# One decoder layer on one core: the out stage goes by token halves, activation sums are made before the transposes, staged weight sums are made sooner

## The chip, the cores and the metric

The kernel runs on one NeuronCore of one Trainium2 chip. The core has five engines, each with its own instruction stream: TensorE (PE; its weight loads are PEld in the profile), VectorE (DVE), ScalarE (ACT), GpSimd (POOL) and SyncE (SP), whose queue issues the DMAs here. The metric is the device time of the one core in microseconds (us).

## The reference

One layer, 1024 tokens, width 1024, all in float32. The parts that this change touches come after the token mixing, which leaves `merged`:

```python
    h = h + rmsnorm(merged @ w_out[i], mix_post_norm[i])
    f = rmsnorm(h, ffn_pre_norm[i])
    f = jnp.square(jax.nn.relu(f @ w_ff_in[i])) @ w_ff_out[i]
    h = h + rmsnorm(f, ffn_post_norm[i])
    e = (p[i] @ w_ple[i]) * jax.nn.sigmoid(h @ w_ple_gate[i])
    h = h + rmsnorm(e, ple_post_norm[i])
```

`w_out` is 1024 x 1024, `w_ff_in` 1024 x 4096, `w_ff_out` 4096 x 1024. `rmsnorm` divides by the root mean square of a row and multiplies by a gain.

## The kernel before

**Arithmetic.** Every float32 operand is split into a high part (fp32r, an ACT copy) and a low part (value minus high, on DVE or POOL), and each product is three matmuls (`mm3`, lines 292, 294, 296): high-high, high-low, low-high. Nearly every other instruction of ACT, DVE, POOL and SP is recorded through a wrapper, at line 113 for the compute engines and 132 for DMAs, so the profile's groups are told apart by tile names.

**Order.** PE's order is made at build time by a planner (`Order`): a list of dense bodies (matmuls) into which chains (generators that wait, then emit a few instructions) are woven by estimated times; `t_f[i]` is the planner's time at which tile `i` of `f` is ready, and `done` its list of events. A wait in it orders the instructions; no engine executes it. PE then works strictly in that order. ACT, DVE, POOL and SP are put in order by the framework, except where `manual_schedule` binds them to the order in which the code names them: SP alone from the start of `mlp`, all four (`OTHERS`) from the mixed pairs on.

**Out stage.** `merged` lies transposed in `mT` (high and low, one tile for each half of the tokens, tags `mth0`, `mtl0`, `mth1`, `mtl1`). `out_0(i)` multiplies token tile `i` (128 tokens) with the left 512 columns of `w_out` (`wo[0]`, in `TM0`, `TM1`) and `out_1(i)` with the right 512 (`wo[1]`, in `AR0`, `AR1`, `BK`, `UV`); each is a body of 24 matmuls of 128x512. All eight `out_0` come first, then all eight `out_1`. Behind each `out_1` the chain `mixed(i)` applies both norms and the residual (`x` is loaded by each `out_1` into `gn["x"]`), stores `h`, and calls `put_f(hh, i)`, which transposes the normalised tile on PE (`tp`) and writes the operands of the first MLP product, `f`. `F[1]` and `F[2]` are the halves of the width of the first 512 tokens; for the second 512 tokens `put_f` writes `F[3]` from the second half of the width, and from both halves the sums `F[4]` to `F[7]`.

**MLP.** Both products of the MLP are done in pairs of blocks by a seven-product scheme (Winograd's form of Strassen): `SEQ` and `MUL` name its products. The pair index `p` runs over 16 (`NP`). `mlp` works so:
- 27 *early* products (`early`, 12 matmuls each) of `F[1]`, `F[2]` with weights `wa` split three products ahead (`w1_split`, from `beside`), results to DRAM. `beside(j)` also makes, once the planner's clock is past `t_f[7]` + 2, steps of `ahead_`: it loads `w_ff_out` rows (`w2r`) for p = 4, 2, 0, forms four sums of blocks (`w2_sums`) and stores each split sum (`bs`, 0.5 MB) to DRAM.
- five *mixed pairs*: one product of p = 0 (`chunks`, `first`) and one early product each.
- for p from 1 to 15, the products of `first(p)` woven into the second MLP product of pair e = p - 1: for even e by `seven` (seven products, 84 matmuls, with `bs` sums fetched back as `duo`), for odd e by `plain` (eight steps `u`, 96 matmuls). Each weave carries 60 matmuls of `first`. In the odd-e loops the sums for the even p that follows are staged: `load_w2(p)`, then `w2_sums(p, 0..5)`, unless p is in `AHEAD` = (4, 2, 0). `take` loads earlier results (`hr`), `part` splits later weights through the `gst` tiles (`gp`, `gph`).

**Tags.** An `rtile` or `mtile` with a tag waits until the last reader of the tag's previous tile is done. The rows of `w_ff_out` for pair p take tags `("r", "k", "MP")[(2p + k) % 3]`, k = 0 and 1. `gst` has two buffers, PSUM has eight banks: `m0`, `m1` for transposes, `z0`, `z1`, `s0` by `zbank`, `s1` to `s3` by `bank`.

Of the kernel before, what the change touches and what calls it, by code (L numbers as in the profile page):

```python
# [244 lines left out]
def layer(ctx: ExitStack, tc: tile.TileContext, x, pT, wz, wup, w_out, wff1, w_ff2, w_ple, w_pleg,  # L245
# [58 lines left out]
    def wait(cond):  # L304
        while not cond():
            yield 0.1
# [930 lines left out]
    def mtile(p, h, shape, name, dt):  # L1237
        return mgpool().tile(shape, dt, name=name, tag=f"mt{p}{h}")
# [99 lines left out]
    def out_0(i):  # L1338
        def body():
            h, ts = tok(i)  # L1340
            if i == 0:
                gn["m"] = rtile([128, D], "gn", "a")
                SY.dma_start(gn["m"], gains[1:2, :].to_broadcast([128, D]))
            if i == 1:
                wo[1] = wo_half(1, GB)
            ps = zbank()
            yield from mm3(ps, [(mT[0][h][:, k, ts], mT[1][h][:, k, ts]) + wo[0][k] for k in range(KT)])
            if i % 2 == 0:
                y0[i // 2] = rtile([128, 2, 512], "y0", ("r", "k", "Ep", "En")[i // 2])
            y = y0[i // 2][:, i % 2]  # L1350
            V.tensor_tensor(y, ps, gn["m"][:, halves[0]], OP.mult)
            jk = rtile([128, 512], "jk", "gst")
            S.activation(jk, ps, AF.Square, accum_out=ss0[:, i:i + 1])
        sch.add(body)

    def out_1(i):
        def body():
            h, ts = tok(i)
            if i == 0:
                gn["f"] = rtile([128, D], "gn", "kk")  # L1360
                SY.dma_start(gn["f"], gains[2:3, :].to_broadcast([128, D]))
                gn["h"] = rtile([128, 2, 2, 512], "hh", "BT")
                gn["x"] = [rtile([128, D], "xt", t) for t in ("v", "px")]
                for n, tag in zip((1, 2), GA):
                    t = rtile([128, 2, 4, 512], "f", tag, F32R)
                    F[n] = t[:, 0], t[:, 1]
            if i in (5, 6):
                mlp_ahead(i - 5)
            ps = zbank()
            SY.dma_start(gn["x"][i % 2], x[i * 128:(i + 1) * 128, :])  # L1370
            yield from mm3(ps, [(mT[0][h][:, k, ts], mT[1][h][:, k, ts]) + wo[1][k] for k in range(KT)])
            sch.spawn(mixed(i, ps), 1)
        sch.add(body)

    gn = {}
    F = {}

    def ss2(srcs, jks):
# [17 lines left out]

    def mixed(i, ps):
        h = i // 4
        yield from wait(lambda: i == 0 or ("M", i - 1) in done and (i < 2 or i - 2 in t_f))
        xt = gn["x"][i % 2]  # L1400
        hh = [gn["h"][:, i % 2, c] for c in range(2)]
# [12 lines left out]
        yield sch.until(sch.dep + 0.3)  # L1414
        yield from wait(lambda: i < 5 or i - 1 in t_f)
        yield from put_f(hh, i)
        t_f[i] = sch.dep + 0.1

    def put_f(srcs, i):


        ts = slice((i % 4) * 128, (i % 4) * 128 + 128)
        if i == 4:
            for n, p, h in ((3, 0, 0), (7, 1, 0), (5, 0, 1), (6, 1, 1)):
                t = mtile("hl"[p], h, [128, 2, 4, 512], "f", F32R)
                F[n] = t[:, 0], t[:, 1]
            F[4] = [rtile([128, 4, 512], "f", tag, F32R) for tag in ("AR0", "AR1")]
        at = lambda n, x: F[n][x][:, :, ts]
        for b in range(2):
            ps, tag = yield from chain_bank([128, 4, 128], "tp")  # L1430
            for k in range(4):
                tr(ps[:, k, :], srcs[b][:, k * 128:(k + 1) * 128], 0.107)
            if i < 4:
                S.activation(at(1 + b, 0), ps, AF.Copy)
                V.tensor_tensor(at(1 + b, 1), ps, at(1 + b, 0), OP.subtract)
            elif b == 0:
                c = rtile([128, 4, 128], "c", "ex")
                S.activation(c, ps, AF.Copy)
            else:
                S.activation(at(3, 0), ps, AF.Copy)  # L1440
                V.tensor_tensor(at(3, 1), ps, at(3, 0), OP.subtract)
                d = rtile([128, 4, 128], "d", "py")
                V.tensor_tensor(d, ps, c, OP.subtract)
            sch.hold(tag)
        if i < 4:
            return
        t2, t4 = (rtile([128, 4, 128], n, tag) for n, tag in (("t2", "pg"), ("t4", "yc")))
        V.tensor_tensor(t2, d, at(1, 0), OP.add)
        V.tensor_tensor(t2, t2, at(1, 1), OP.add)
        G.tensor_tensor(c, c, at(1, 0), OP.subtract)  # L1450
        G.tensor_tensor(c, c, at(1, 1), OP.subtract)
        G.tensor_tensor(t4, at(2, 0), t2, OP.subtract)
        G.tensor_tensor(t4, t4, at(2, 1), OP.add)
        for n, x, eng in ((7, d, V), (6, t2, V), (5, c, G), (4, t4, G)):
            if n in (6, 5):
                yield 2.0
            S.activation(at(n, 0), x, AF.Copy)
            eng.tensor_tensor(at(n, 1), x, at(n, 0), OP.subtract)

    NP = FF // 256
    MUL = (1, 6, 5, 3, 7, 4, 2)
# [5 lines left out]

    def totals():  # L1470
        for m in range(2):
            t = rtile([128, 2, 4, 512], "tot", GA[m])
            tot.append([t[:, 0], t[:, 1]])

    def acc(i, c):
# [200 lines left out]
    def mlp():  # L1676
# [2 lines left out]
        while sch.t < t_f.get(3, 1e9):  # L1679
            yield 0.0  # L1680
        for j in range(NA):
            beside(j)
            yield from early(j)
        while sch.t < t_f.get(7, 1e9):
            yield 0.0
        last["turn"].__exit__(None, None, None)
        last["turn"] = tc.manual_schedule(engines=OTHERS)
        last["turn"].__enter__()
        A_["turn"] = True
        for n in range(5):  # L1690
            beside(NA + 2 * n)
            yield from chunks(4 * n + 4)
            beside(NA + 2 * n + 1)
            Y["j"] += 1
            yield from early(NA + 2 * n + 1)
            flush()
        prep(0)
        prep(1)
        for _ in range(4):
# [1 line left out]
        for p in range(1, NP):  # L1701
            Y["n"] = 0
            e = p - 1
            if e % 2 == 0:
                for x in range(7):
                    yield from chunks((20 * x + 23) // 7 if p < NP - 1 else (3, 6, 9, 13, 17, 20, 20)[x])
                    yield from seven(items.index((e, x)))
                    if x == 2:
                        load_w2(p)
                    if x == 4:  # L1710
                        take(p + 1)
                    if p == NP - 1:
# [11 lines left out]
            for u in range(8):  # L1724
# [1 line left out]
                    flush()  # L1726
                    part(2 * p - 4 + u // 2, 0)
                yield from chunks((20 * u + 23) // 8)
                if u == (2 if p in AHEAD else 0):
                    load_w2(p)  # L1730
                yield from plain(items.index((e, u // 2)), u % 2)
                if u == 3:
                    take(p + 1)
                if p in AHEAD:
                    if u == 3:
                        fetch(p, 6)
                else:
                    if u == 1:
                        w2_sums(p, 0)
                    if 0 < u < 6:  # L1740
                        w2_sums(p, u)
                if u % 2:
                    part(2 * p - 4 + u // 2, 1)
        for _ in range(4):
# [234 lines left out]
            P[f"p{n - 2}"] = [k2(t[:, 0]), k2(t[:, 1])]  # L1979

    def last_weights():
        P["wpg"] = [[mtile("hl"[p], 1 - c, [128, KT, 512], "wpg", F32R) for c in range(2)] for p in range(2)]
        P["g3"] = rtile([128, D], "g3", "v")
        SY.dma_start(P["g3"], gains[3:4, :].to_broadcast([128, D]))

# [244 lines left out]
```

## Time and profile before

| | us |
|---|---|
| median of 3 runs | 1799.94 (1799.66 to 1800.44) |
| the profiled execution | 1800.09 |
| its span in the profile | 1798.3 |
| out stage, first to last matmul of `w_out` | 895.7 to 988.7 |
| early products and mixed pairs, to the first `bk<-duo` | 988.7 to 1118.0 |
| `seven` and `plain`, to the last MLP pair | 1118.0 to 1651.9 |

Positions are from the span's start. In a row of the timeline stand start, duration, engine, line, operation, out<-in and count, and in brackets the idle time before it and what ended it. A matmul's duration includes its pipeline; what it costs in a dense row is the distance to the next start. A row of waits says which engine waited, for whom, how long in total, how often, and the longest.

### The profile page before, as it was taken

Reading aid. Unit: us, or ns where it says so; the run is one execution under the profiler, and the core shown is the slowest. Engines: PE = TensorE matmul, PEld = TensorE weight load, DVE = VectorE, ACT = ScalarE, POOL = GpSimd, SP = SyncE. Lnnn points to the kernel's source line nnn. Section 1 sums busy time; section 2 is a strip of 40 time slices with the busy share of each in tenths; the row PEclk is TensorE's granted clock in tenths of the full one; section 3 lists DMA queues with packets and bytes.
Section 4 is the critical chain, followed back from the end, with each engine's and each line's share of the span. In section 5 each row is a group of like instructions: output and inputs, shape, how many; then the busy total and the mean of one; then the engine's idle time right before and its main releaser. Section 6 shows DMA issues by size and latency. Waiting matters only on the chain.

```text
span 1798.3 us, 26359 instructions
## 1 busy us (share of the span) xinstructions
PE 1741.8 (97%) x10084; PEld 1410.6 (78%) x10084; DVE 1100.8 (61%) x1873; ACT 753.1 (42%) x1377; POOL 682.1 (38%) x458
## 2 busy tenths in 40 slices
PE   9999989999999999999999898999999999999998
PEld 8887877878877777778878686888878777787887
DVE  6289767677534333353727745766776777778743
ACT  5824433432344443543515565343333433334453
POOL 1344131231221323332310854665655656553211
PEclk9999999999999999999999999999999999999999
DMA  4621121213332222333504378554464464657611
GB/s 160 208 94 37 48 82 48 90 45 106 111 107 79 69 63 60 106 138 132 205 29 141 115 271 298 170 180 165 148 228 167 167 212 154 214 181 276 245 48 47
DMA packets 99969, 244.76 MB, mean 136 GB/s; under 512 B 11394, under 2 KB 11778, under 8 KB 99331
## 3 DMA queue, kind: packets, MB, share of 16 engines
q1 hardware_dynamic: 99842, 243.08, 39.3%
q8 instruction: 79, 1.29, 0.3%
q14 instruction: 48, 0.39, 0.1%
HBM read 169.24 MB, written 67.11 MB: 131 GB/s over the span
## 4 chain that ended last, share of the span: by engine, by line
PE 66%; DVE 9%; DMA 9%; ACT 5%; POOL 4%; issue 4%; SPq 2%; DVEq 0%; ACTq 0%; POOLq 0%
PE z L294 13%; PE z L296 13%; PE z L292 13%; PE bk L292 5%; PE bk L294 5%; PE bk L296 5%; SPq L132 2%; DMA w2r<-in_w_ff_dram 1%; DVE tot L113 1%; DMA duo<-bs 1%; PE sc L275 1%; DMA wa<-in_wff_dram 1%; DVE xy L113 1%; PE A L275 1%; PE y L275 1%
## 5 line engine op out<-in xcount | busy, mean ns | idle before, releaser
L292 PE MATMUL z<-uh,wh 128*128 128x512 f32 (+1 forms) x800 | 313.0, 391 | 6.2 <-ACT part L113 3.0
L294 PE MATMUL z<-ul,wh 128*128 128x512 f32 (+1 forms) x800 | 314.6, 393 | 1.3 <-DVE ul L113 1.3
L296 PE MATMUL z<-uh,wl 128*128 128x512 f32 (+1 forms) x800 | 313.3, 392 | 2.7 <-POOL wl L113 2.7
L113 POOL TENSOR_TENSOR wl<-wr,wh 128x1024 fp32r<-128x1024 f32 (+1 forms) x56 | 133.4, 2382 | 421.1 <-ACT wh L113 402.1
L113 DVE TENSOR_TENSOR tot<-tot,bk 128x512 f32<-128x512 f32 x336 | 219.6, 680 | 65.7 <-PE bk L296 65.4
L292 PEld LDWEIGHTS z<-uh,wh 128*128 128x128 f32 x800 | 151.5, 189 | 37.2 <-ACT part L113 3.5
L296 PEld LDWEIGHTS z<-uh,wl 128*128 128x128 f32 x800 | 151.6, 189 | 34.1 <-POOL wl L113 4.0
L294 PEld LDWEIGHTS z<-ul,wh 128*128 128x128 f32 x800 | 151.7, 190 | 32.4 <-issue 3.6
L113 ACT ACTIVATE wh<-wr 128x1024 fp32r<-128x1024 f32 (+2 forms) x94 | 81.0, 862 | 113.0 <-PE z L294 56.2
L113 ACT ACTIVATE hr<-hr 128x512 f32<-128x512 f32 x96 | 60.7, 632 | 133.2 <-DVE hr L113 131.7
L292 PE MATMUL bk<-duo 128*128 128x512 f32 x224 | 91.4, 408 | 14.9 <-DMA duo<-bs 8.9
L113 ACT ACTIVATE duo<-sum 128x512 fp32r<-128x512 f32 x64 | 40.0, 625 | 123.2 <-DVE sum L113 122.6
L294 PE MATMUL bk<-duo 128*128 128x512 f32 x224 | 89.6, 400 | 0.2 <-POOL duo L113 0.2
L296 PE MATMUL bk<-duo 128*128 128x512 f32 x224 | 89.4, 399 | 0.0
L292 PE MATMUL bk<-ws,duo 128*128 128x512 f32 x224 | 87.1, 389 | 0.0
L294 PE MATMUL bk<-ws,duo 128*128 128x512 f32 x224 | 87.1, 389 | 0.0
L296 PE MATMUL bk<-ws,duo 128*128 128x512 f32 x224 | 87.1, 389 | 0.0
L292 PE MATMUL z<-f,wh 128*128 128x512 f32 x212 | 83.1, 392 | 2.2 <-ACT pa L113 2.2
L296 PE MATMUL z<-f,wh 128*128 128x512 f32 x212 | 83.0, 392 | 0.0
L294 PE MATMUL z<-f,wh 128*128 128x512 f32 x212 | 82.9, 391 | 0.0
L113 POOL TENSOR_TENSOR wh<-wr,wh 128x512 fp32r<-128x512 f32 x38 | 53.9, 1421 | 67.3 <-ACT wh L113 55.8
L292 PEld LDWEIGHTS bk<-duo 128*128 128x128 f32 x224 | 43.3, 193 | 32.7 <-DVE tot L113 13.0
(366 smaller groups left out, 4113.3 us busy)
## 6 DMA issues: line engine op xcount, KB each, us to landing
wr<-in_wz_dram SPq DMA_DIRECT2D x48, 512.0 KB, 3.8
w2r<-in_w_ff_dram SPq DMA_DIRECT2D x34, 512.0 KB, 6.3
bs<-duo SPq DMA_DIRECT2D x32, 512.0 KB, 4.1
duo<-bs SPq DMA_DIRECT2D x32, 512.0 KB, 5.1
wr<-in_wff_dram SPq DMA_DIRECT2D x56, 256.0 KB, 4.1
hr<-p1scr SPq DMA_DIRECT2D x48, 256.0 KB, 4.7
xt<-in_x_dram SPq DMA_DIRECT2D x16, 512.0 KB, 3.7
gscr<-gst SPq DMA_DIRECT2D x32, 256.0 KB, 2.1
```

Of the source, the lines that this page charges most:

```text
L113: return f(*a, **kw)
L132: self.eng.dma_start(out_, in_)
L275: PE.matmul(out_, a, b, start=start, stop=stop)
L292: PE.matmul(ps, ah, bh, start=start and i == 0, stop=False, skip_group_check=not start)
L294: PE.matmul(ps, ah, bl, start=False, stop=False, skip_group_check=not start)
L296: PE.matmul(ps, al, bh, start=False, stop=i == n - 1, skip_group_check=not start)
```

## The change

- The bodies run as `out_0(0..3)`, `out_1(0..3)`, then `out_0(i)`, `out_1(i)` in turn for i = 4 to 7. `wo[1]` is prepared one body sooner, `out_0` takes its bank from `bank`, and `x` is loaded two tiles ahead from `mixed`.
- Each tile's normalised activations have a room of their own (`room_h`) instead of one of two. `F[1]`, `F[2]` and the totals `tot` move to the tags of `mT`'s first half, `F[3]`, `F[7]` to `TM0`, `TM1`; `wpg` follows.
- `put_f` for tiles 4 to 7 forms the sums in fp32 on the untransposed tiles `hhs[i - 4]` and `srcs`, and transposes all five operands; it no longer sums transposed operands. The transposes of a half are placed behind that half's last `out_1`.
- `ACT`, `DVE` and `POOL` are bound to the written order only after the five mixed pairs instead of before them.
- In `plain` loops the load for a p outside `AHEAD` moves to the end of the `seven` loop before, its six sum steps from u = 1, 1 to 5 to u = 0 to 3; `take` moves from u = 3 to 4, and the first `bs` fetch of such a p to u = 5.

```diff
@@ out_0 @@
-            if i == 1:
                 wo[1] = wo_half(1, GB)
-            ps = zbank()
+            ps = bank()
@@ out_1 @@
-                gn["h"] = rtile([128, 2, 2, 512], "hh", "BT")
+                hh = rtile([128, 2, 2, 512], "hh", "BT")
+                gn["h"] = [[hh[:, n, c] for c in range(2)] for n in range(2)]
...
-            if i in (5, 6):
-                mlp_ahead(i - 5)
+                for n in range(2):
+                    load_rows(n)
+            if i in (6, 7):
+                mlp_ahead(i - 6)
             ps = zbank()
-            SY.dma_start(gn["x"][i % 2], x[i * 128:(i + 1) * 128, :])
...
+            done.add(("O", i))
+    def load_rows(i):
+        SY.dma_start(gn["x"][i % 2], x[i * 128:(i + 1) * 128, :])
+    def room_h(i):
+        if i < 2:
+            return gn["h"][i]
+        if i in (3, 4):
+            return [rtile([128, 512], "hh", t) for t in (("ex", "py"), ("pg", "yc"))[i - 3]]
+        t = rtile([128, 2, 512], "hh", {2: "MP", 5: "r", 6: "k", 7: "Ep"}[i])
+        return [t[:, 0], t[:, 1]]
@@ mixed @@
-        yield from wait(lambda: i == 0 or ("M", i - 1) in done and (i < 2 or i - 2 in t_f))
+        yield from wait(lambda: i == 0 or ("M", i - 1) in done)
...
+        if i < 6:
+            load_rows(i + 2)
         yield sch.until(sch.dep + 0.3)
-        yield from wait(lambda: i < 5 or i - 1 in t_f)
+        yield from wait(lambda: (i == 0 or i - 1 in t_f) and ("O", 7 if i > 3 else 3) in done)
@@ put_f @@
+        if i == 0:
+            for n, p in ((1, 0), (2, 1)):
+                t = mtile("hl"[p], 0, [128, 2, 4, 512], "f", F32R)
+                F[n] = t[:, 0], t[:, 1]
...
-        t2, t4 = (rtile([128, 4, 128], n, tag) for n, tag in (("t2", "pg"), ("t4", "yc")))
-        V.tensor_tensor(t2, d, at(1, 0), OP.add)
-        V.tensor_tensor(t2, t2, at(1, 1), OP.add)
-        G.tensor_tensor(c, c, at(1, 0), OP.subtract)
-        G.tensor_tensor(c, c, at(1, 1), OP.subtract)
-        G.tensor_tensor(t4, at(2, 0), t2, OP.subtract)
-        G.tensor_tensor(t4, t4, at(2, 1), OP.add)
-        for n, x, eng in ((7, d, V), (6, t2, V), (5, c, G), (4, t4, G)):
...
+        todo = [(1, srcs[0]), (2, srcs[1])]
+        if i > 3:
+            a, b = hhs[i - 4], srcs
+            t2 = rtile([128, 512], "t2", "gst")
+            V.tensor_tensor(a[0], b[0], a[0], OP.subtract)
+            V.tensor_tensor(b[0], b[1], b[0], OP.subtract)
+            V.tensor_tensor(t2, b[1], a[0], OP.subtract)
+            G.tensor_tensor(a[1], a[1], t2, OP.subtract)
+            todo = [(3, b[1]), (5, a[0]), (7, b[0]), (6, t2), (4, a[1])]
+        for n, src in todo:
+            o = (slice(None), slice(None), ts)
             ps, tag = yield from chain_bank([128, 4, 128], "tp")
             for k in range(4):
+                tr(ps[:, k, :], src[:, k * 128:(k + 1) * 128], 0.107)
+            S.activation(F[n][0][o], ps, AF.Copy)
+            V.tensor_tensor(F[n][1][o], ps, F[n][0][o], OP.subtract)
             sch.hold(tag)
@@ beside @@
         if j == 20:
+            yield from wait(lambda: 7 in t_f)
             take(0)
@@ mlp @@
         while sch.t < t_f.get(7, 1e9):
             yield 0.0
+        for n in range(5):
+            yield from beside(NA + 2 * n)
+            yield from chunks(4 * n + 4)
+            yield from beside(NA + 2 * n + 1)
+            Y["j"] += 1
+            yield from early(NA + 2 * n + 1)
+            flush()
         last["turn"].__exit__(None, None, None)
         last["turn"] = tc.manual_schedule(engines=OTHERS)
         last["turn"].__enter__()
-        A_["turn"] = True
-        for n in range(5):
...
+                    if x == 6 and p < NP - 1 and p + 1 not in AHEAD:
+                        load_w2(p + 1)
...
-                if u == (2 if p in AHEAD else 0):
+                if u == 2 and p in AHEAD:
                     load_w2(p)
                 yield from plain(items.index((e, u // 2)), u % 2)
-                if u == 3:
+                if u == 4:
                     take(p + 1)
-                if p in AHEAD:
-                    if u == 3:
-                        fetch(p, 6)
-                else:
-                    if u == 1:
-                        w2_sums(p, 0)
-                    if 0 < u < 6:
-                        w2_sums(p, u)
+                if u == (3 if p in AHEAD else 5):
+                    fetch(p, 6)
+                if p not in AHEAD:
+                    for n in ((0,), (1, 2), (3, 4), (5,), (), (), (), ())[u]:
+                        w2_sums(p, n)
@@ end of layer @@
-    for i in range(8):
+    for i in range(4):
         out_0(i)
-    for i in range(8):
+    for i in range(4):
+        out_1(i)
+    for i in range(4, 8):
+        out_0(i)
         out_1(i)
```

More of the change, by code (lines that the diff above doesn't have):

```diff
@@ L1361, in body @@
                 SY.dma_start(gn["f"], gains[2:3, :].to_broadcast([128, D]))
-                gn["h"] = rtile([128, 2, 2, 512], "hh", "BT")
+                hh = rtile([128, 2, 2, 512], "hh", "BT")
+                gn["h"] = [[hh[:, n, c] for c in range(2)] for n in range(2)]
                 gn["x"] = [rtile([128, D], "xt", t) for t in ("v", "px")]
-                for n, tag in zip((1, 2), GA):
-                    t = rtile([128, 2, 4, 512], "f", tag, F32R)
-                    F[n] = t[:, 0], t[:, 1]
-            if i in (5, 6):
-                mlp_ahead(i - 5)
+                for n in range(2):
+                    load_rows(n)
+            if i in (6, 7):
+                mlp_ahead(i - 6)
             ps = zbank()
-            SY.dma_start(gn["x"][i % 2], x[i * 128:(i + 1) * 128, :])
             yield from mm3(ps, [(mT[0][h][:, k, ts], mT[1][h][:, k, ts]) + wo[1][k] for k in range(KT)])
             sch.spawn(mixed(i, ps), 1)
+            done.add(("O", i))
         sch.add(body)
+    def load_rows(i):
[7 more added lines that the diff above has]
+        return [t[:, 0], t[:, 1]]
     gn = {}
+    hhs = {}
     F = {}
@@ L1398, in mixed @@
         h = i // 4
-        yield from wait(lambda: i == 0 or ("M", i - 1) in done and (i < 2 or i - 2 in t_f))
+        yield from wait(lambda: i == 0 or ("M", i - 1) in done)
         xt = gn["x"][i % 2]
-        hh = [gn["h"][:, i % 2, c] for c in range(2)]
+        hh = hhs[i] = room_h(i)
         ss = small.tile([128, 1], F32, name="ss")
@@ L1422, in put_f @@
         ts = slice((i % 4) * 128, (i % 4) * 128 + 128)
+        if i == 0:
+            for n, p in ((1, 0), (2, 1)):
+                t = mtile("hl"[p], 0, [128, 2, 4, 512], "f", F32R)
+                F[n] = t[:, 0], t[:, 1]
         if i == 4:
-            for n, p, h in ((3, 0, 0), (7, 1, 0), (5, 0, 1), (6, 1, 1)):
-                t = mtile("hl"[p], h, [128, 2, 4, 512], "f", F32R)
+            for n, t in ((3, rtile([128, 2, 4, 512], "f", "TM0", F32R)), (7, rtile([128, 2, 4, 512], "f", "TM1", F32R)),
+                         (5, mtile("h", 1, [128, 2, 4, 512], "f", F32R)), (6, mtile("l", 1, [128, 2, 4, 512], "f", F32R))):
@@ L1426, in put_f @@
                 F[n] = t[:, 0], t[:, 1]
             F[4] = [rtile([128, 4, 512], "f", tag, F32R) for tag in ("AR0", "AR1")]
-        at = lambda n, x: F[n][x][:, :, ts]
-        for b in range(2):
+        todo = [(1, srcs[0]), (2, srcs[1])]
[7 more added lines that the diff above has]
+            todo = [(3, b[1]), (5, a[0]), (7, b[0]), (6, t2), (4, a[1])]
@@ L1430, in put_f @@
+        for n, src in todo:
+            o = (slice(None), slice(None), ts)
             ps, tag = yield from chain_bank([128, 4, 128], "tp")
             for k in range(4):
[L1432 to L1438, printed above, removed]
-            else:
[L1440 to L1443, printed above, removed]
@@ L1444, in put_f @@
-            sch.hold(tag)
-        if i < 4:
-            return
-        t2, t4 = (rtile([128, 4, 128], n, tag) for n, tag in (("t2", "pg"), ("t4", "yc")))
-        V.tensor_tensor(t2, d, at(1, 0), OP.add)
-        V.tensor_tensor(t2, t2, at(1, 1), OP.add)
-        G.tensor_tensor(c, c, at(1, 0), OP.subtract)
-        G.tensor_tensor(c, c, at(1, 1), OP.subtract)
-        G.tensor_tensor(t4, at(2, 0), t2, OP.subtract)
-        G.tensor_tensor(t4, t4, at(2, 1), OP.add)
-        for n, x, eng in ((7, d, V), (6, t2, V), (5, c, G), (4, t4, G)):
[L1455 to L1458, printed above, removed]
+                tr(ps[:, k, :], src[:, k * 128:(k + 1) * 128], 0.107)
@@ L1471, in totals @@
         for m in range(2):
-            t = rtile([128, 2, 4, 512], "tot", GA[m])
+            t = mtile("hl"[m], 0, [128, 2, 4, 512], "tot", F32)
             tot.append([t[:, 0], t[:, 1]])
@@ L1681, in mlp @@
         for j in range(NA):
-            beside(j)
+            yield from beside(j)
             yield from early(j)
@@ L1688, in mlp @@
         last["turn"].__enter__()
-        A_["turn"] = True
-        for n in range(5):
[L1691 to L1696, printed above, removed]
         prep(0)
@@ L1981, in last_weights @@
     def last_weights():
-        P["wpg"] = [[mtile("hl"[p], 1 - c, [128, KT, 512], "wpg", F32R) for c in range(2)] for p in range(2)]
+        P["wpg"] = [[rtile([128, KT, 512], "wpg", "TM1", F32R), mtile("h", 1, [128, KT, 512], "wpg", F32R)],
+                    [mtile("l", 1, [128, KT, 512], "wpg", F32R), rtile([128, KT, 512], "wpg", "TM0", F32R)]]
         P["g3"] = rtile([128, D], "g3", "v")
```

1 line of the change is left out of this document (removed).

## The prediction

> **What bounds the kernel now.** I read the page first, then the waits of TensorE, then stretches around the change.
>
> ```profile
> span 1798.3 us, 26359 instructions
> PE 1741.8 (97%) x10084; PEld 1410.6 (78%) x10084; DVE 1100.8 (61%) x1873; ACT 753.1 (42%) x1377; POOL 682.1 (38%) x458
> ```
>
> TensorE (PE) works in its written order and is busy 97%, so only two things move the time: the number of its instructions, and the places where it stands. The second view is busy time by stretch (PE, weight loads, DVE, ACT, POOL, granted clock, DMA share, GB/s): the out stage, the early products, the stretch in which the staged sums are made, and the mixed products up to the first product of `seven`. The single row under it is PE alone over the last three.
>
> ```profile
> 895.68:988.68 93.00, 91.60 (x424) 75.89 (x423) 46.43 (x82) 32.58 (x85) 11.85 (x6) 1.00 0.28 92
> 988.68:1050.00 61.32, 52.74 (x223) 41.42 (x223) 41.86 (x40) 34.68 (x71) 52.49 (x35) 0.94 0.37 126
> 1050.00:1098.00 48.00, 48.00 (x212) 39.36 (x211) 23.17 (x31) 27.44 (x49) 14.34 (x11) 1.00 0.97 351
> 1098.00:1118.04 20.04, 14.03 (x48) 9.62 (x46) 11.61 (x12) 12.46 (x24) 11.87 (x9) 0.87 0.67 258
> ```
> ```profile
> 988.68:1118.04 129.36, 114.77 (x480) 0.95 0.64 230
> ```
>
> The out stage has POOL nearly idle (11.85 us) and PE nearly full; the stretch behind it has POOL at 52.49 of 61.32 us and PE standing. How much is lost there: nine matmuls lie between the next two starts, (1324.20 - 1322.16) / 9 = 0.2267 us each.
>
> ```profile
> 1322.16 0.39 PE L292 MATMUL z<-f,wh 128*128 128x512 f32 x1
> 1324.20 0.39 PE L292 MATMUL bk<-duo 128*128 128x512 f32 x1
> ```
> ```profile
> 954.95 1.03 PE L283 MATMUL tp<-cs,hh 128*128 128x128 f32 x8
> 955.74 0.47 PE L296 MATMUL z<-wo,mt 128*128 128x512 f32 x1
> 956.05 0.39 PE L292 MATMUL z<-wo,mt 128*128 128x512 f32 x1
> ```
>
> Eight transposes put 956.05 - 954.95 - 0.2267 = 0.87 us between matmuls, 0.109 each. Up to 1118.04 the code has 27 early products, five pairs and nine matmuls of the next: 37 x 12 + 9 = 453 matmuls, and 24 transposes (x480 less these and the edges agrees). That is 102.7 + 2.6 = 105.3 us, so about **24 us of 129.4 are lost**. Waits of PE there, and one of them in order of time:
>
> ```profile
> PE bk L292 <- ACT wh L113: 3.8, 1, 3.8
> PE bk L292 <- ACT pa L113: 3.7, 1, 3.7
> PE bk L296 <- POOL wh L113: 2.3, 3, 1.1
> ```
> ```profile
> 1013.84 0.80 PE L292 MATMUL bk<-f,wl 128*128 128x512 f32 x1 [3.66 <-ACT pa L113]
> 1014.43 0.63 PE L294 MATMUL bk<-f,wl 128*128 128x512 f32 x1
> ...
> 1016.99 0.53 PE L294 MATMUL bk<-f,wl 128*128 128x512 f32 x1
> ```
>
> Seven steps behind this wait, from 1013.84 to 1016.99, take 3.15 us instead of 1.59 (the granted clock of 0.94 and 0.87 above is their trace): a long stall costs its own length and some 1.6 us more. What POOL spends from 980 to 1055 on the operations that read or write `f` (busy us, count, clock, DMA):
>
> ```profile
> 980.00:1055.00 75.00, 37.29 (x24) 0.95 0.40 135
> ```
>
> That is `put_f` of tiles 4 to 7, six operations a tile, 1.55 us each; the weight lows that PE waits for (`wh`, `wl`) queue behind them, and ACT, which must also empty `pa`, stands for POOL's `c` and `t`. From 1098 it is the staged sums: their loads, stores and splits fill the DMA engines (share 0.97 above) and the queues of DVE and ACT.
>
> Later the same wait returns at five places. First products of `seven` for p = 4 and p = 14 (p = 6 stands above, at 1324.20), PE's waits from 1118.1 to 1660, and those from 1619 to 1640:
>
> ```profile
> 1255.84 0.39 PE L292 MATMUL bk<-duo 128*128 128x512 f32 x1
> ...
> 1619.32 0.39 PE L292 MATMUL bk<-duo 128*128 128x512 f32 x1
> ```
> ```profile
> PE bk L292 <- DMA duo<-bs: 8.9, 4, 2.6
> PE bk L292 <- DVE tot L113: 5.7, 11, 1.2
> ```
> ```profile
> PE bk L292 <- DVE tot L113: 1.4, 2, 1.2
> ```
>
> From p = 4, whose sums were staged ahead, to p = 6 is 68.36 us; the next four pairs take 1619.32 - 1324.20 = 295.12, and 4 x 68.36 = 273.44. **21.7 us are lost**, 5.4 a pair; the fifth boundary, behind 1619, adds 1.4. Two waits make these: bank copies late on DVE, and the third product's operand, fetched late.
>
> **The change, part by part.**
>
> *Order of the out stage.* The same 384 matmuls. `wo_half(1)` is issued one body sooner, but its tiles hold `orw` until the last merge. The half is needed after four bodies instead of eight, 4 x 24 x 0.2267 = 21.8 us after the stage's start; its lows are done 13 us after it:
>
> ```profile
> L113 POOL TENSOR_TENSOR wo<-wr,wo x4: 2396/2626/2859, 895.0 to 905.9; 128x1024 fp32r<-128x1024 f32 x4
> ```
>
> Nothing is lost. The six residual loads that follow the first two are issued by `mixed`, two tiles ahead, and past nothing that waits. I take 0, and 1 us either way for the low that PE waits for at the stage's start.
>
> *Norm chains.* They run beside the out stage, 10.9 us a tile for the second half instead of 5.4, so tiles 4 to 6 are normalised when it ends; before, tiles 5 to 7 fell behind it. Their DVE and ACT work leaves the crowded stretch. The transposes of tiles 0 to 3 are placed behind the last body of their half (their `f` now lies where `mT` of that half lay), hidden: only the early products want them. Those of tiles 4 to 7 are placed behind all 16 bodies, in front of which nothing waits.
>
> *Sums before the transposes.* Removed per tile of the second half: six POOL operations, 37.3 us in all, and their ACT and DVE partners. Added: three DVE subtractions, one on POOL (1.6 us), and five groups of four transposes instead of two, each with an ACT copy and a DVE subtraction. PE pays 48 transposes x 0.109 = **+5.2 us**, on the path. Durations:
>
> ```profile
> L283 PE MATMUL tp<-cs,hh x64: 270/272/418, 955.0 to 1034.5; 128*128 128x128 f32 x64
> L113 ACT ACTIVATE f<-tp x12: 578/590/601, 955.6 to 1034.8; 128x512 fp32r<-128x512 f32 x12
> L113 DVE TENSOR_TENSOR f<-tp,f x12: 677/686/692, 956.4 to 1035.4; 128x512 fp32r<-128x512 f32 x12
> ```
> ```profile
> 988.10 0.69 DVE L113 TENSOR_TENSOR t<-d,f 128x512 f32<-128x512 f32 x1
> ...
> 990.41 1.77 DVE L113 TENSOR_TENSOR t<-t,f 128x512 f32<-128x512 f32 x1
> ```
>
> DVE needs 3 x 0.69 + 5 x 0.686 = 5.5 us a tile, 8.7 where POOL runs beside the three sums (1.77). Four tiles are 22 to 35 us, beside 27 early products of 2.72 us (73 us): covered, if PE isn't sent to transposes whose source isn't there. Behind such a transpose the early products queue. Bounds: 0, and 4 x (8.7 - 5.5) = 13 us. I take 3 us, near the lower, because POOL falls in that stretch from 52.5 us to 52.5 - 37.3 + 4 x 1.6 = 22.
>
> The Trainium skill, "TensorE: Matmul & The Clock Gate", section "Part 4: PE-mode transpose", speaks against this part: a transpose takes some 275 ns inside a kernel, and the clock monitor doesn't count it as work. By its figure the sum would be 8 us higher. The trace has the same 272 ns, but as a latency: the eight above follow each other at 0.109, and the matmul behind them is at the full step again.
>
> *Staged sums sooner, first half.* The ahead sums of p = 4, 2, 0 start when tile 7 is done. In the code's order that was step 20 of 27 (their first load leaves at 1065.58). Now tile 7 should be done some 25 us into the early products (four tiles by 5.5 us, and a little for its norm), about step 10, and the sums end before the mixed products:
>
> ```profile
> 1065.58 0.94 SPq L132 DMA_DIRECT2D w2r<-in_w_ff_dram  x2
> ```
>
> DMA issues from 1058 to 1100, then from 988 to 1050 (count, size, median us to landing):
>
> ```profile
> DMA packets 6672, 15.38 MB, mean 366 GB/s; under 512 B 745, under 2 KB 745, under 8 KB 6667
> ...
> bs<-duo SPq DMA_DIRECT2D x8, 512.0 KB, 6.6
> w2r<-in_w_ff_dram SPq DMA_DIRECT2D x6, 512.0 KB, 7.3
> wa<-in_wff_dram SPq DMA_DIRECT2D x8, 256.0 KB, 6.4
> ```
> ```profile
> wa<-in_wff_dram SPq DMA_DIRECT2D x14, 256.0 KB, 3.5
> ```
>
> Six loads and twelve stores of 0.5 MB move from a full stretch (366 GB/s) into one at 126 GB/s (its row above). Beside weights and partial products (0.5 MB per 2.72 us) they make about 400 GB/s for 16 products, again full; `wa` then lands in 6.4 us instead of 3.5 and has 8.2 (three products). I take 1 us of new waits for it (0 to 6).
>
> *With one answer, nothing:* other tags for `f`, `tot` and `wpg` (the same sizes, freed by the same products or one earlier); `bank` for `out_0`, so that the norm chains keep the three `z` banks; ACT, DVE and POOL leave the written order for the five pairs, where PE's 24 us include some of the strict order's waits; `take` one step later, with its first use a whole step on. Each is covered by the slack named; if `take` were late, DVE's first `hr` would wait, not PE.
>
> So this stretch: -24 + 5.2 + 3 + 1 = **-15 us**.
>
> *Staged sums sooner, second half.* For p = 6 to 14 the load moves from the first step of `plain` to the end of the `seven` before, and the sums from steps 1 to 5 to steps 0 to 3. The queue of SP, POOL and DVE around p = 6:
>
> ```profile
> 1294.56 0.90 SPq L132 DMA_DIRECT2D w2r<-in_w_ff_dram  x2
> ```
> ```profile
> 1288.95 2.56 POOL L113 TENSOR_TENSOR ws<-w2r,ws 128x512 fp32r<-128x512 f32 x2 [3.17 <-ACT ws L113]
> ```
> ```profile
> 1300.40 0.69 DVE L113 TENSOR_TENSOR sum<-w2r 128x512 f32<-128x512 f32 x1 [3.88 <-DMA w2r<-in_w_ff_dram]
> ```
>
> DVE stands for the load, and everything behind slips by some 5 us until the fetch that the third product of `seven` needs. Of the two rows loaded, the second takes the tag of the previous p's first, which POOL reads until about 1290.2; SP waits there, and only a `gp` load stands behind it. It lands some 4.5 us sooner, as the sums come up: the DVE wait goes, and four steps of 4.4 us (156 matmuls in eight steps) are left to catch up. The new wait is for a store: the third split takes the room of the first, stored about one step before; ACT may stand up to 3 us, still caught up. Gain 0 to 23.2; I take 20, near the p = 4 row, which has no stall with its sums done ahead.
>
> The sum: 1800.09 (this execution; its span and 1.8 around it; the median of the runs, 1799.94, is the same to 0.01%) - 15 - 20 = **1765 us**.
>
> **The rivals.**
> - *Transposes ahead of their sources.* DVE at 8.7 us a tile, PE standing 13 us and losing clock once a tile (4 x 1.6): 19 us in place of the 3 in the sum, so the first gain goes: 1800 + 1 - 20 = 1781. For: contention rows of 1.77. Against: POOL's work is halved.
> - *The load isn't sooner.* SP and DVE wait for the `ws` read as they did for the queue: 1785. For: the tag rule above. Against: 1290.2 is before 1294.56.
> - *Transposes at their latency*: alone between other work each costs its median, 48 x 0.272 = 13 us instead of 5.2: 1773. For: groups are of four now, more often cut off. Against: the eight in 0.87 us. (The rule of Part 4 of the page on TensorE in the Trainium skill would give this.)
> - *No new wait at all*: -24 + 5.2 and -23.2, 1758.
> - *Slower: SP's queue.* A store of a sum waits for DVE, and the weight loads wait behind it:
>
> ```profile
> 1102.85 6.80 SPq L132 DMA_DIRECT2D bs<-duo  x2
> ```
>
> Six such pairs among the early products are 41 us, less 8.2 of lead, and 6 x 1.6 of clock: 42 us against 35 gained, 1807. It decides once two blocks fall within 8.2 us. Against: before, eight stores were issued from 1058 to 1100 and PE didn't stand.
> - *Nothing*: the stalls have other owners and the extra transposes pay for what goes: 1800.
>
> **How the numbers follow.** Forecast 0.50; transposes ahead 0.14; load not sooner 0.12; no new wait 0.10; latency 0.05; slower 0.05; nothing 0.04. The range 1755 to 1787 leaves out slower, nothing and the tails of the others. Faster by over 0.2% (3.6 us, about what a measurement of this kernel can tell): 0.91; within: 0.04; slower: 0.05.
>
> **What would show it.** 112 transposes instead of 64. POOL under 30 us between the out stage and the first `bk<-duo`, which comes near 1103. Clock 1.00 there. `w2r` loads from about 1020. Pairs of `seven` 68 to 70 us apart from p = 6 on, no `DVE sum` waiting for `w2r`, no PE waiting for `duo<-bs`. Pairs still 74 apart would sink the second term; PE waiting at `tp` would sink the first.

## The result, and the profile after

| | before | after |
|---|---|---|
| median, us | 1799.89 (4 runs, 1799.66 to 1800.44) | 1782.2 (4 runs, 1775.91 to 1784.11) |
| the profiled execution, us | 1800.09 | 1784.11 |
| ratio, 95% interval | | 0.9895 (0.987 to 0.992) |

The change makes the kernel 17.7 us faster. The forecast of 1765 was 17 us too low; the time lies in its range. Most of this section asks which half of the forecast was not paid.

The head of the page after:

```profile
span 1782.3 us, 26426 instructions
PE 1738.8 (98%) x10132; PEld 1415.0 (79%) x10132; DVE 1087.3 (61%) x1881; ACT 752.3 (42%) x1373; POOL 649.3 (36%) x438
```

48 more matmul records, 20 fewer of POOL, and a span 16.0 us shorter. Where these came from is read from positions of PE. Busy time of PE by stretch (start and end, length, busy, count, clock, DMA share, GB/s), first before, then after. The four stretches run from the start of the out stage to the first product of `seven` for p = 0, then for p = 6, then for p = 14, then to the first matmul with `lw` (the weights of the last MLP pair):

```profile
895.68:1118.04 222.36, 206.37 (x903) 0.97 0.49 172
1118.04:1324.20 206.16, 205.84 (x901) 1.00 0.51 174
1324.20:1619.32 295.12, 281.77 (x1201) 0.98 0.53 185
1619.32:1651.92 32.60, 31.19 (x136) 1.00 0.68 243
```
```profile
898.72:1110.15 211.43, 205.74 (x950) 0.99 0.51 183
1110.15:1315.19 205.04, 204.91 (x901) 1.00 0.52 178
1315.19:1603.99 288.80, 277.99 (x1202) 0.99 0.55 190
1603.99:1636.91 32.92, 30.76 (x136) 1.00 0.65 235
```

The out stage starts 3.0 us later, behind code that the change doesn't touch. The four stretches give -10.9, -1.1, -6.3 and +0.3, and what is behind them -1.0 (146.4 before, 145.4 after). The sum is -16.0. Against the forecast, the first stretch gives 10.9 of 15; the third, which was to give nearly all of 20, gives 6.3.

**The first stretch.** All engines over the early products and the rest (PE, weight loads, DVE, ACT, POOL, clock, DMA share, GB/s), and two of the waits of PE, the longest and that for `tp`:

```profile
991.72:1050.00 58.28, 57.70 (x293) 47.78 (x292) 36.53 (x50) 38.91 (x75) 21.59 (x16) 1.00 0.56 198
1050.00:1110.15 60.15, 56.42 (x239) 45.60 (x238) 25.29 (x31) 33.75 (x59) 27.33 (x21) 0.97 0.81 299
```
```profile
PE bk L292 <- ACT wh L113: 1.6, 1, 1.6
...
PE tp L283 <- DVE f L113: 0.5, 1, 0.5
```

In the early products POOL has 21.59 us of work where it had 52.49, PE stands for nearly nothing (57.70 busy of 58.28) and the clock is 1.00. Counted as in the prediction, 453 matmuls x 0.2267 and 80 transposes x 0.109 are 111.4 us, and 1110.15 - 991.28 is 118.9: 7.5 us are lost instead of 24. The one long stall left is for `wh` near 1069: ACT waits for sums that POOL couldn't start, as their raw weights land late. POOL and ACT in order of time:

```profile
1065.18 1.29 POOL L113 TENSOR_TENSOR sum<-wr 128x512 f32<-128x512 f32 x1 [14.39 <-DMA wr<-in_wff_dram]
```
```profile
1069.28 0.63 ACT L113 ACTIVATE wh<-wr 128x512 fp32r<-128x512 f32 x1 [3.46 <-POOL wr L113]
```

**The third stretch.** The largest wait of PE from 1112 to 1640, then SP, DVE, ACT and PE around the start of p = 6, whose first product stands at 1315.19:

```profile
PE bk L292 <- DMA duo<-bs: 10.1, 4, 2.7
```
```profile
1271.32 10.28 SPq L132 DMA_DIRECT2D w2r<-in_w_ff_dram  x2
...
1317.78 0.32 SPq L132 DMA_DIRECT2D pkl<-gph  x1
1318.50 0.32 SPq L132 DMA_DIRECT2D pkl<-gp  x1
1319.68 1.28 SPq L132 DMA_DIRECT2D wr<-in_wff_dram  x3
1321.01 0.43 SPq L132 DMA_DIRECT2D duo<-bs  x1
```
```profile
1285.27 1.18 DVE L113 TENSOR_TENSOR sum<-w2r 128x512 f32<-128x512 f32 x1
```
```profile
1297.09 0.63 ACT L113 ACTIVATE duo<-sum 128x512 fp32r<-128x512 f32 x1 [8.21 <-DMA bs<-duo]
```
```profile
1327.45 0.47 PE L292 MATMUL bk<-duo 128*128 128x512 f32 x1 [2.57 <-DMA duo<-bs]
```

DVE's first sum has no wait for `w2r` any more, and the waits for `DVE tot` (5.7 us before) are gone. But the third product still stands 2.57 us for its operand: the fetch leaves at 1321.01, 5.8 us behind the first product. Before the change it was 8.0, against the start at 1324.20:

```profile
1332.18 0.38 SPq L132 DMA_DIRECT2D duo<-bs  x1
```

Two things in these rows could hold it. ACT stands 8.21 us for a store; and in SP's queue the fetch stands behind two stores of `gp` parts and three loads of the first weights. From 1309 to 1322 SP itself waits longest for ACT's copy of the part that the first of these stores writes out:

```profile
SPq L132 <- ACT gph L113: 4.0, 2, 3.4
```

The place in the queue is not late by itself. At p = 4, whose first product is at 1246.82, the same fetch stands behind the same stores, leaves 1.95 us behind the first product, and PE doesn't wait. The first of the two stores there, and the fetch:

```profile
1245.08 0.32 SPq L132 DMA_DIRECT2D pke<-gph  x1
...
1248.77 0.43 SPq L132 DMA_DIRECT2D duo<-bs  x1
```

There the store leaves 1.7 us ahead of the first product, at p = 6 it leaves 2.6 us behind it. The first five experiments ask what the fetch's place costs, and what the store that ACT waits for.

### The profile page after: what moved, and what is told of

The parts are those of the page before. It is cut to its first block, busy times and chain, and to the rows that moved or that the text cites. A ratio compares the mean times of both kernels' runs of the same rounds, so it can differ in the third digit from the quotient of the medians.

```text
span 1782.3 us, 26426 instructions
## 1 busy us (share of the span) xinstructions
PE 1738.8 (98%) x10132; PEld 1415.0 (79%) x10132; DVE 1087.3 (61%) x1881; ACT 752.3 (42%) x1373; POOL 649.3 (36%) x438
## 4 chain that ended last, share of the span: by engine, by line
PE 80%; DVE 8%; ACT 4%; DMA 4%; issue 3%; POOL 1%; SPq 0%; DVEq 0%; ACTq 0%; POOLq 0%
PE z L294 14%; PE z L292 14%; PE z L296 14%; PE bk L292 8%; PE bk L296 8%; PE bk L294 8%; DMA duo<-bs 1%; PE tp L283 1%; PE sc L275 1%; DVE xy L113 1%; PE A L275 1%; PE y L275 1%; PE po L275 1%; PE pt L283 1%; PE wr L275 1%
## 5 line engine op out<-in xcount | busy, mean ns | idle before, releaser
L292 PE MATMUL bk<-duo 128*128 128x512 f32 x224 | 89.5, 399 | 10.4 <-DMA duo<-bs 10.1
L296 PE MATMUL bk<-duo 128*128 128x512 f32 x224 | 88.3, 394 | 0.0
L294 PE MATMUL bk<-duo 128*128 128x512 f32 x224 | 88.3, 394 | 0.0
L113 DVE TENSOR_TENSOR hr<-hr,z 128x512 f32<-128x512 f32 x80 | 54.4, 680 | 20.1 <-PE z L296 19.9
```

What stands on the lines that cost most here:

```text
L113: return f(*a, **kw)
L292: PE.matmul(ps, ah, bh, start=start and i == 0, stop=False, skip_group_check=not start)
L294: PE.matmul(ps, ah, bl, start=False, stop=False, skip_group_check=not start)
L296: PE.matmul(ps, al, bh, start=False, stop=i == n - 1, skip_group_check=not start)
```

## The experiments

Ratios are to runs of the kernel before that were made beside each kernel (medians 1799.28 to 1801.62), with 95% intervals; kernels are compared by them. "Lost" for the pairs is the distance from the first product of `seven` for p = 6 to that for p = 14, less 4 x 68.36. The first stretch is that from the first matmul of the out stage to the first `bk<-duo`. Both are from one profile each. Kernels whose code is the changed kernel's in the first stretch (after, a0, x1 to x5) lie between 209.2 and 212.4 there, those whose code is the same in the pairs (after, a0, y1 to y4) lose 13.0 to 17.1: smaller differences mean nothing. Where an expectation speaks of the first product of `seven` for p = 4 at 1103 to 1110, the position is that for p = 0 (1110.15 in the changed kernel).

| kernel | median, us | ratio | lost in four pairs | first stretch |
|---|---|---|---|---|
| before | 1799.89 | | 21.7 | 222.4 |
| after | 1782.2 | 0.9895 (0.987 to 0.992) | 15.4 | 211.4 |
| after, again (a0) | 1779.43 | 0.9875 (0.9845 to 0.9906) | 17.1 | 212.4 |
| early fetch (x1) | 1770.7 | 0.9817 (0.9795 to 0.984) | 0.9 | 209.2 |
| fifth and sixth sum later (x2) | 1784.27 | 0.9907 (0.9881 to 0.9933) | 16.0 | 209.5 |
| first half alone (x3) | 1791.35 | 0.9938 (0.9917 to 0.9959) | 23.6 | 212.2 |
| x1 and x2 (x4) | 1767.36 | 0.9807 (0.9786 to 0.9828) | 1.4 | 209.2 |
| first half, early fetch (x5) | 1778.55 | 0.9877 (0.9852 to 0.9902) | 9.6 | 210.7 |
| ahead sums from step 20 (y1) | 1780.25 | 0.9895 (0.9869 to 0.992) | 13.0 | 211.1 |
| old order of the out stage (y3) | 1788.61 | 0.9942 (0.9922 to 0.9962) | 15.5 | 218.2 |
| sums after transposes (y4) | 1795.29 | 0.9978 (0.9962 to 0.9994) | 16.3 | 225.8 |
| strict order for the five pairs (y2) | 1783.8 | 0.9904 (0.9873 to 0.9936) | 13.1 | 209.9 |
| x4, weights sooner (y5) | 1771.07 | 0.9827 (0.9799 to 0.9856) | 2.3 | 209.8 |

**x1: the fetch ahead in SP's queue.**

```diff
                 yield from plain(items.index((e, u // 2)), u % 2)
+                if u == 7:
+                    fetch(p, 5)
```

> The changed kernel, and the fetch of the third product's operand (i = 5) is issued right behind the last step of plain, ahead of the stores of gp and the loads of the first weights in SP's queue. Theory A (the 15.4 us that four pairs still lose, 288.8 instead of 4 x 68.36, are the late fetch; its lateness is its place in SP's queue, behind the stores of gp): the waits of PE for duo<-bs go, pairs take 68 to 70 us, 1766 to 1770. Rival B (the sums themselves are late because ACT stands 8.2 us for the store of the first room; the fetch can't leave until they are stored): half of the waits at most go, 1776 to 1782. Rival C (the bank copies, not the fetch, cost the pairs): 1781 to 1784.

The ratio falls from 0.9895 to 0.9817, and the waits for `duo<-bs` are gone. SP's queue around p = 6, whose first product is at 1308.53 here, and ACT just before:

```profile
1307.38 0.39 SPq L132 DMA_DIRECT2D duo<-bs  x1
1311.03 0.32 SPq L132 DMA_DIRECT2D pkl<-gph  x1
...
1312.93 2.84 SPq L132 DMA_DIRECT2D wr<-in_wff_dram  x4
```
```profile
1290.34 0.63 ACT L113 ACTIVATE duo<-sum 128x512 fp32r<-128x512 f32 x1 [8.13 <-DMA bs<-duo]
```
```profile
1308.53 0.39 PE L292 MATMUL bk<-duo 128*128 128x512 f32 x1
...
1582.88 0.39 PE L292 MATMUL bk<-duo 128*128 128x512 f32 x1
```

The fetch leaves 1.2 us ahead of the first product instead of 5.8 behind it, and four pairs take 274.35 us. ACT still stands 8.13 us for the store, and with the fetch ahead it costs nothing. Theory A holds (its 1766 to 1770 is missed by 0.7); C is out, and so is B in the form given here, as the fetch leaves in time although ACT's wait is as long as before.

**x2: a shorter wait for the store.** The fifth sum goes one step later, the sixth another.

```diff
-                    for n in ((0,), (1, 2), (3, 4), (5,), (), (), (), ())[u]:
+                    for n in ((0,), (1, 2), (3,), (4,), (5,), (), (), ())[u]:
```

> The changed kernel, and of the six sums of a pair the fifth (n = 4) is made one step later, when the store out of its room should be done, and the sixth a step later still. Theory A (place in SP's queue): ACT's wait of 8.2 us for bs<-duo goes, DVE's and ACT's queues are no longer 5 us late, but the fetch still stands behind the stores of gp and leaves less than 2 us sooner: 1778 to 1784. Rival B (ACT's wait for the store keeps everything behind it late, and the fetch with it): the waits of PE for duo<-bs go, 1767 to 1772.

No gain. ACT's wait is shorter, and SP sends the fetch as late as ever:

```profile
1291.92 0.63 ACT L113 ACTIVATE duo<-sum 128x512 fp32r<-128x512 f32 x1 [4.93 <-DMA bs<-duo]
```
```profile
1316.83 0.43 SPq L132 DMA_DIRECT2D duo<-bs  x1
```

The first product is at 1310.13, the fetch 6.7 us behind it. But this is no clean test of rival B: 4.93 us of ACT's wait are left, and SP now stands for a store of its own, ahead of the fetch of another sum (from 1297 to 1307):

```profile
SPq L132 <- DMA bs<-duo: 6.5, 1, 6.5
```

What rules B out is x1. Whether ACT's wait is among what makes the `gp` stores late at p = 6 is not shown.

**x3: the first half of the change alone.**

```diff
-                    if x == 6 and p < NP - 1 and p + 1 not in AHEAD:
-                        load_w2(p + 1)
...
-                if u == 2 and p in AHEAD:
+                if u == (2 if p in AHEAD else 0):
...
-                    for n in ((0,), (1, 2), (3, 4), (5,), (), (), (), ())[u]:
+                    for n in ((), (0, 1), (2,), (3,), (4,), (5,), (), ())[u]:
```

(`take` and the fetch of i = 6 go back too.)

> The first half of the change alone: order of the out stage, norm chains, sums ahead of transposes, ahead sums; the load, the sums, the take and the fetch of the pairs p = 6 to 14 at the steps where they were before. If the two halves are separate, as the prediction has it, the pairs take 73.8 us again (21.7 and 1.4 lost instead of 15.4) and the second half is worth 6 to 8 us: 1788 to 1791, with the first products of seven for p = 4 near 1110 as in the changed kernel. The prediction's own figure for the second half, 20, would give 1802. A rival, that the two halves share a cause (the DMA queue), would give 1782 to 1785.

0.9938: the first half alone is worth 11 us, and the second half another 8 to 11 (0.9938 less 0.9895 and 0.9875, each known to some 4 us either way), not 20. The pairs lose 23.6 us, as before the change, by both waits:

```profile
PE bk L292 <- DMA duo<-bs: 9.8, 5, 2.8
PE bk L292 <- DVE tot L113: 7.1, 10, 1.5
```

**x4: both edits.** x1 and x2 together.

> Both edits of the two runs before: the early fetch, and the fifth and sixth sums a step later each. Theory A: as with the early fetch alone, 1765 to 1770. Rival B: as with the sums a step later alone, 1767 to 1772. If the two are two waits one behind the other, each alone gives half or less, and this one all of it, 1764 to 1768.

0.9807, the fastest of all and not to be told from x1: with the fetch in place, the store's wait has nothing to add. The profiled execution took 1764.6 us.

**x5: the early fetch without the earlier load and sums.** The edits of x3 and of x1.

> The first half of the change alone with the early fetch of i = 5 (the loads and sums of the pairs p = 6 to 14 where they were before). If the place in SP's queue was all that the pairs lost, the earlier load and sums are worth nothing beside it and the pairs take 68 to 70 us here as well: 1766 to 1771. If the sums must also be sooner, because in the old order DVE's wait of 3.9 us for the load keeps them late whatever SP's order is, some of the waits for duo<-bs or for the bank copies stay: 1774 to 1784.

0.9877, in the second case. The waits for `duo<-bs` are gone even with the old load and sums; what is left is the bank copies alone, since DVE still stands for the load (waits of PE from 1122 to 1640, and DVE):

```profile
PE bk L292 <- DVE tot L113: 6.7, 10, 2.0
```
```profile
1289.87 0.69 DVE L113 TENSOR_TENSOR sum<-w2r 128x512 f32<-128x512 f32 x1 [3.94 <-DMA w2r<-in_w_ff_dram]
```

So the loss of the pairs has two owners that are nearly independent. From x3, the earlier load and sums alone take it from 23.6 to 15.4, the early fetch alone to 9.6, both to 0.9.

**y1: the ahead sums where they were.**

```diff
-        if sch.t > t_f.get(7, 1e9) + 2.0:
+        if j > 19 and sch.t > t_f.get(7, 1e9) + 2.0:
```

> The changed kernel, but the sums made ahead (p = 4, 2, 0) start at step 20 of the early products, as they did before, instead of when tile 7 is done (about step 11). The prediction puts most of the 24 us to POOL's work for the last tiles and to these sums together. If the sums' place matters (loads, stores and splits in the full stretch from 1050 on), the first product of seven for p = 4 comes 4 to 10 us later and the time is 1786 to 1792. If POOL's work alone made the loss, within 2 us of the changed kernel: 1780 to 1784.

The same ratio as the changed kernel: the `w2r` loads leave from 1056.54 on instead of 1035.42, and the first stretch is 211.1 instead of 211.4. The stall for `wh` goes, one of 3.3 us for `pa` comes:

```profile
PE z L292 <- ACT pa L113: 3.3, 1, 3.3
```

Making these sums sooner was worth nothing by itself.

**y3: the old order of the out stage.**

```diff
-    for i in range(4):
+    for i in range(8):
         out_0(i)
-    for i in range(4):
-        out_1(i)
-    for i in range(4, 8):
-        out_0(i)
+    for i in range(8):
         out_1(i)
```

> The changed kernel with the old order of the out stage: all eight first column halves, then all eight second ones. The prediction puts the order itself at 0 but says that the norms of the last tiles then fall behind the stage. If that is so, the transposes of tiles 5 to 7 come later and some of them wait, and the sums ahead begin some 5 us later: 1785 to 1790. If the order matters for nothing: 1780 to 1784. A store of more: the transposes of tiles 0 to 3 can't be hidden in the stage, as their buffers come free at its end only: 1790 to 1796.

0.9942, some 8 us slower than the changed kernel; 6.8 of them lie in the first stretch. The two largest waits of PE in it, and the longest one for `tp`:

```profile
PE tp L283 <- DVE f L113: 5.0, 4, 2.9
PE z L292 <- ACT pa L113: 3.7, 1, 3.7
```
```profile
1009.75 1.12 PE L283 MATMUL tp<-cs,hh 128*128 128x128 f32 x4 [2.92 <-DVE f L113]
```

With the old order, PE is sent to transposes whose banks DVE hasn't emptied: a form of the prediction's first rival happens here (PE waits for the bank, not for the source), and the new order is what keeps it out of the changed kernel (0.5 us there). It is not all of the 6.8 us: the wait for `pa`, near 1109, has 1.0 us in the changed kernel, and those for `wh` near 1069 are nearly gone. Why `pa` comes late was not traced to the order.

**y4: activation sums made from the transposed tiles, as before.** `put_f` has its old sums back, with `c`, `d`, `t2` and `t4`. These need their tiles again, so token tiles 3 and 4 go back to the two shared rooms; the rest is the changed kernel.

> The changed kernel with the sums of activations made as before, from the transposed tiles (two groups of transposes a tile instead of five, and six operations of POOL a tile back). It has 48 transposes less, 5.2 us by the prediction's price. If POOL's work made the loss in the early products (the prediction), its 37 us come back where the weight lows queue: 5 to 15 us of waits for wh and wl, less 5.2: 1782 to 1793. If POOL wasn't the cause, the transposes alone count and it is faster: 1776 to 1779.

0.9978: nearly the whole gain is gone, and 1795.29 is 2 us above the range expected. POOL's operations on `f` from 980 to 1055 (busy, count), the two largest waits of PE up to 1126, and the largest of ACT from 985 to 1075:

```profile
980.00:1055.00 75.00, 36.56 (x24) 0.93 0.33 107
```
```profile
PE bk L292 <- ACT wl L113: 5.3, 2, 4.1
PE z L292 <- ACT pa L113: 4.6, 1, 4.6
```
```profile
ACT f L113 <- POOL t L113: 13.0, 4, 3.7
```

The 36.56 us of POOL are back. ACT stands 13.0 us for POOL's `t` (10.1 before the change, nothing in the changed kernel), and behind it in ACT's queue are the weight splits that PE waits for. The stretch is 14.4 us longer than in the changed kernel although it has 48 transposes less: the old sums cost PE 14.4 + 5.2 = 19.6 us. Two limits: 3.6 of it are the wait for `pa` near 1121, which has 1.0 us in the changed kernel but 3.3 in y1 as well, and was not traced to the sums; and y4 brings back the ACT and DVE work of the old sums with POOL's, so the 19.6 us belong to them together.

**y2: the strict order for the five pairs.** The three lines that enter `manual_schedule(OTHERS)` go back ahead of the loop.

> The changed kernel with ACT, DVE and POOL held to the written order for the five pairs of products again, as before the change. The prediction put this part at nothing, with a doubt (some of the 24 us lost could be waits of the strict order). If nothing: 1780 to 1784. If the strict order costs waits for the sums made ahead: the first product of seven for p = 4 comes 3 to 8 us later, 1785 to 1791.

0.9904, and a first stretch of 209.9: nothing that can be told from the changed kernel, as predicted.

**y5: x4 with the late weights sooner.**

```diff
-        if j in (18, 19):
-            w1_raw(0, *((21, 11) if j == 18 else (22, 12)))
+        if j in (12, 13):
+            w1_raw(0, *((21, 11) if j == 12 else (22, 12)))
```

> The kernel with the early fetch and the later fifth and sixth sums, and the four loads of the first weights of p = 0 at steps 12 and 13 of the early products instead of 18 and 19, ahead of most of the loads and stores of the sums. If the 2.9 us lost near 1065 (PE waits for ACT wh, ACT for POOL's sums, POOL 12.9 us for these loads) come from their place behind the sums' stores in full DMA queues: the stall goes, 1761 to 1765. If the loads are late wherever they stand, or the loads displaced wait in turn: no change, 1765 to 1768.

No gain (1771.07, above both ranges; 0.9827 against 0.9807 of x4 can't be told apart). POOL no longer waits for the weights, but its four sums now run beside the sums made ahead on DVE, whose operations take up to 1.77 us there, and PE waits for a weight low behind them:

```profile
PE bk L296 <- DVE wl L113: 2.5, 2, 1.7
```

**a0: the changed kernel once more.**

> The changed kernel once more, unaltered, for its spread and a second profile. The first product of seven for p = 4 is at 1103 to 1110 in the runs so far whose code up to there is the same, and the stretches of 2.2 to 2.7 us in which PE waits for duo<-bs are followed by slow steps at some pairs and not at others: 1776 to 1784, and another share of the pairs with slow steps.

The time is as expected; the first product of `seven` for p = 0 stands at 1111.80, 1.8 us past the range. The slow steps are taken up in the last section.

## Why the prediction was right and wrong

- **Direction and range: right, the range in part by luck.** Both halves gain, by 11 and by 8 to 11 us of the 15 and 20 forecast. The part of the range where 1782 lies was there mainly for two rivals (1781 and 1785) whose mechanisms did not happen.
- **POOL's work as the owner of the 24 us: right in the main.** Putting the old sums back (y4) costs up to 19.6 us of PE, and with them the stretch loses some 27 us, where it lost 24 before. POOL acts on PE mostly through ACT, which stands for POOL's `t` ahead of the weight splits. The residue was 7.5 us instead of 4. The sign "POOL under 30 us between the out stage and the first `bk<-duo`" was a slip: it is 21.59 + 27.33 = 48.9, since the last 60 us have other work; the forecast of 22 was for the early products, and there it is 21.59.
- **48 transposes at 0.109 us: right.** Eight of them lie between these starts, 992.07 - 991.05 - 0.2267 = 0.79 us in all:

```profile
991.05 0.40 PE L292 MATMUL bk<-f,wh 128*128 128x512 f32 x1
991.28 1.03 PE L283 MATMUL tp<-cs,hh 128*128 128x128 f32 x8
992.07 0.47 PE L294 MATMUL bk<-f,wh 128*128 128x512 f32 x1
```

- **Transposes ahead of sources, 3 us taken: 0.5 us of waits.** The order of the out stage, for which the prediction says "I take 0", is what earns this: without it these waits are 5.0 us and the time is 8 us longer, for `tp` and `pa` together (y3). The prediction had the mechanism under norm chains, but no price for it.
- **Ahead sums "end before the mixed products": wrong, and without effect.** They start 15 us later than the forecast 1020, their stores run into the mixed pairs, and their place doesn't matter (y1).
- **No cost for leaving the strict order: right** (y2).
- **Second half, 20 us: the step that failed.** The prediction let one chain explain the lost 21.7 us: "DVE stands for the load, and everything behind slips by some 5 us until the fetch that the third product of `seven` needs". The load does come sooner, DVE's wait does go, and with it the loss by the bank copies. The fetch comes only 2.2 us sooner (5.8 us behind the first product instead of 8.0): in SP's written order it stands behind the stores of the `gp` parts and the loads of the next first weights. x1 shows it: one fetch moved past them takes the loss from 15.4 to 0.9 us. x5 shows that the fetch didn't cost PE for DVE's sake: with the old load and the old sums, moving it alone ends the waits for `duo<-bs`. The prediction asked what would be late next and named a store ("The new wait is for a store"); it did not follow SP's queue on to the fetch. The pair of p = 4, from which the 20 was taken, has the fetch at the same place in the queue and loses nothing, as the stores ahead of it leave some 4 us sooner there. What makes them late from p = 6 on stays open.
- **The store's wait: wrong in size.** The "up to 3 us" were 8.21. With the fetch moved they cost nothing (x1); without that, x2 doesn't tell.
- **The rivals.** "The load isn't sooner" (1785) came nearest in time, but not by its mechanism: SP is held 10.28 us for the `ws` read, as it says, yet DVE doesn't wait. SP's queue as the slower rival didn't show among the early products; it is the same queue, at another place, that kept 14 us of the gain (0.9895 less 0.9817).

What stays open: the 3.0 us by which the out stage starts later in the changed kernel's profile. It isn't the change's doing, as kernels with the same code up to there start it between 894.26 (x1) and 899.93 (y2); why was not looked into.

## What to carry to other kernels

Where a wait for a DMA is to go, read the whole queue that issues it: a transfer whose data is ready early still leaves at its place in a written order, behind stores that wait for other engines. Compare with a place where the same transfer is in time: here the queue's order was the same, and what stood ahead was later. A long wait of a side engine (8 us of ACT here) is no cause until the chain from it to the bound engine is shown. Two edits, each alone and together, tell two owners of a loss apart. Work taken off an engine that is free most of the time (POOL, busy 38%) can be worth far more than what replaces it costs on the bound engine: 37 us of POOL, with the ACT and DVE work that went with them, were worth up to 20 us of PE, for 5 us of transposes.

## What the runs showed of the hardware

A stall of 2.2 to 2.9 us doesn't always cost the slow steps that the prediction charged with it (1.6 us). In the changed kernel two of the four waits for `duo<-bs` are followed by seven or eight steps of 0.43 us, in its second profile three. The steps behind the wait of 2.57 us shown above (0.24 us, none slow), those behind a longer one (slow after 1.5 us), and, from the second profile, those behind the shortest one, where they begin at once:

```profile
1327.75 0.40 PE L294 MATMUL bk<-duo 128*128 128x512 f32 x1
1327.99 0.39 PE L296 MATMUL bk<-duo 128*128 128x512 f32 x1
...
1399.47 0.47 PE L292 MATMUL bk<-duo 128*128 128x512 f32 x1 [2.68 <-DMA duo<-bs]
...
1400.94 0.63 PE L292 MATMUL bk<-duo 128*128 128x512 f32 x1
```
```profile
1328.84 0.77 PE L292 MATMUL bk<-duo 128*128 128x512 f32 x1 [2.21 <-DMA duo<-bs]
1329.41 0.63 PE L294 MATMUL bk<-duo 128*128 128x512 f32 x1
```

The length of the wait doesn't decide it: 2.21 us has the slow steps, 2.57 us has none, and in x2 a wait of 2.96 us has none either. The same wait in the same code comes with and without them. Ahead of the first matmul with `lw` PE stands 2.15 to 2.17 us in the changed kernel and in every experiment; only in x1 do slow steps follow, and there the part behind takes 147.0 us instead of 145.4 or 145.5.

The Trainium skill, "TensorE: Matmul & The Clock Gate", section "Part 1: The HAM clock gate", tells of a free-running window of about 3.4 us, so that the phase varies from run to run. A slow stretch of some 3 us (seven steps of 0.43) that comes or stays away would agree with that; no run here shows the window itself. The page says that the clock falls after an idle window of about 3.4 us. Here the steps are slow behind a wait of 2.2 us, and the measurement decides.
